# Mixture of 16,384 single-neuron experts: dense products with the whole tables, replaced by gathered rows per block of 128 tokens

## The chip, the cores and the metric

The kernel runs on one core of a Trainium2 chip. Its engines are TensorE (PE; products and transposes, results to PSUM), VectorE (DVE), ScalarE (ACT), GpSimd (POOL) and SyncE (SP, which here only issues DMAs); 16 DMA engines move data between HBM and SBUF. The metric is the device time of one execution in microseconds; the median of three runs before the change is 5664.9 us (5652.19 to 5668.03).

## The reference, cut to what matters

One layer of a backbone with 128 context tokens and 512 latent tokens, each of 2048 channels in float32. A token mixer (input projection, state-space scan, two convolutions, merge, output projection) is followed by PEER, a mixture of 16,384 experts of one neuron each. The change is in PEER:

```python
q = (xt @ p["peer_w_q"]).reshape(tok, PEER_HEADS, 2, PEER_QDIM // 2)   # 8 heads, two halves of 128
s1 = einsum("thd,nd->thn", q[:, :, 0], peer_k1)     # 128 first keys
s2 = einsum("thd,nd->thn", q[:, :, 1], peer_k2)     # 128 second keys
v1, i1 = top_k(s1, 16);  v2, i2 = top_k(s2, 16)
cand = v1[..., :, None] + v2[..., None, :]          # 256 sums a head
cidx = i1[..., :, None] * 128 + i2[..., None, :]    # expert = 128 * first key + second key
top, sel = top_k(cand.reshape(tok, 8, 256), 16)
idx = take_along_axis(cidx, sel);  g = softmax(top)
# per token: 8 heads x 16 = 128 experts
act = einsum("cd,ckd->ck", xc, u_tab[idx])          # u_tab, v_tab: [16384, 2048]
out = einsum("ck,ckd->cd", g * gelu(act), v_tab[idx])
```

The result is gated, added to the residual and normalised.

## The kernel before, in words

The token mixer comes first (`start`, `project`, `merge`); the change leaves it alone. `peer` (L1294) then works through blocks of 128 tokens: block 0 is the context, blocks 1 to 4 are the latents. Blocks 2, 3, 4 go as one group and 1, 0 as another through the output projection (`wo`, L933), the residual and LayerNorms (`norms`, which transposes the experts' input at L290) and the queries (`queries`, L610 and the scores at L973). Float32 products are made of three: an operand is split into a rounded part (h, ScalarE) and the rest (l, VectorE or GpSimd), and h·h, h·l and l·h are summed. `piece` (L165 to L175) loads 4 KB a partition of a weight and splits it (L173, L174).

`choose` (L1009) takes, for a block, the top 16 keys of each half (L1003 to L1007), the top 16 of their sums and the softmax (to L1048). For latents it then spreads the weights over all experts by products of one-hot rows: 64 steps of two tokens each (L1075 to L1095), into G in DRAM, [32, 16, 128, 128], in four writes of 2 MB a block (L1082).

For the latents, the experts are dense: for each first key e, `up` multiplies all 512 latents with the 128 rows of U of that key (48 products of 512 columns, L610) and takes the gelu; `weigh` multiplies by G; `down` (L1198) adds W^T V for four first keys at a time (L1210), 16 accumulations in PSUM that VectorE adds to `acc` (L1216). Fifty of the 128 `up` steps run ahead, beside the choosing (AHEAD). For the context, `gathers` (L1112) fetches one expert row a token and step by an indirect DMA that GpSimd issues (L1108), 128 rows of U and then of V, and VectorE does the arithmetic (L1124, L1131). `finish_context` and `finish_latents` end it.

The order on each engine comes from a scheduler that goes by the order of the program and its own estimates of time; it may put an instruction that is ready ahead of an earlier one that is not. Waits stand in each engine's instruction stream, in order.

Of the kernel before, what the change touches and what calls it, by code (L numbers as in the profile page):

```python
# [6 lines left out]
F32 = mybir.dt.float32  # L7
# [9 lines left out]
D = 2048  # L17
KT = 16
# [7 lines left out]
# columns of the constants  # L26
C_ID, C_IOTA, C_LOW, C_UP, C_ONES = 0, 128, 256, 384, 512
C_N = 640

# [39 lines left out]
def layout(i):  # L69
    """The device arrays: slices, transposes and copies of the inputs, and constants."""  # L70
# [3 lines left out]
    o["cst"] = consts()  # L74
    o["pos"] = grid_pos()
# [36 lines left out]
    o["put"] = A(n["peer_u"][0].reshape(128, 128, 2, 8, 128).transpose(0, 2, 4, 3, 1))  # L112
# [3 lines left out]
# steps of the gathered experts after each key of a group  # L116
UPS = (2, 2, 1, 0)
# after which pieces of the first adaLN weights the steps of the input come: a block's LN0 (b) and its turning (t),
# the parameters of S5 (p), a quarter of the projection's input and the first products with it (q)
# [4 lines left out]
class Quarters(list):  # L124
    """A tensor [128, 16, NT] in four tiles."""
# [6 lines left out]
class Kern:  # L132
# [8 lines left out]
    # ---- pools  # L141
# [22 lines left out]
    # ---- weights: raw piece of 4 KB a partition, its rounded part and the exact rest  # L164
# [16 lines left out]
    # ---- adaLN vectors; seq 0 is the context, seq 1 the latents  # L181
# [16 lines left out]
    def mod_chunk(self, n, ps, rp=None, tag="m", tb=4):  # L198
        """512 columns of the adaLN vectors; yields between its parts."""
# [37 lines left out]
    def late_mod(self, ps):  # L237
        """The vectors that the input projection does not need, in parts between its products."""
# [3 lines left out]
    # ---- 1/sqrt(var + eps) on DVE and ACT with one Newton step  # L242
# [15 lines left out]
    def ln_stats(self, pool, x):  # L258
        """The mean and 1 / deviation of the rows x [128, 2048]."""
# [8 lines left out]
    def ln_rows(self, pool, x, out):  # L268
        """out = LN0(x) for rows x [128, 2048]."""
# [3 lines left out]
    def x_rows(self, pool, b, x):  # L273
        """Block b of the layer's input into x: context, or latents with their grid positions."""
# [8 lines left out]
    def modulate_T(self, pool, ps, xn, seq, v, h, l, t0, tag, tb):  # L283
        """h, l [128, 16, t] at t0: the split of (xn * (1 + sc) + sh)^T; v is the index of sh."""
# [17 lines left out]
    def start(self):  # L302
# [5 lines left out]
        # LN0 of the input, transposed, by quarters of the channels; its modulated form, split, takes the rest of  # L308
        # the room and then that of the quarters that are done
# [59 lines left out]
        # shift and scale of a quarter of the channels, then that quarter of the projection's input  # L369
        # and of its first products; a chunk is finished under the next one's products  # L370
# [53 lines left out]
    def cmul(self, P, out, a, b, shape, tag, eng=None):  # L424
        """out = a * b for [128, 2, ...] complex tiles (given as (re, im) pairs)."""
# [12 lines left out]
    def s5_params(self, P):  # L438
# [18 lines left out]
        # sin and cos with the angle brought into [-pi, pi]  # L457
# [17 lines left out]
        # PW[e + 4] = a^e for e = -4 .. 11  # L475
# [16 lines left out]
        # z = (a - 1) / lambda  # L492
# [20 lines left out]
        # a^8 twice, the starting slots of the latents and a^3  # L513
# [8 lines left out]
        # powers by position in the chunk: for B, for C inside the chunk, for C on the state  # L522
# [6 lines left out]
        # scratch in DRAM, by blocks of 4 groups  # L529
# [64 lines left out]
    # ---- input projection: 128 columns of it, transposed, into two PSUM tiles of 320 tokens  # L594
# [6 lines left out]
    def mm_T(self, acc, hl, xh, xl, cols, kpp, fill=None):  # L601
        """acc[n] (128 columns, tokens) = sum over the pieces of w^T x, three products a term."""
# [15 lines left out]
    # the two sequences side by side with zeros around them, for depthwise convolutions  # L618
# [6 lines left out]
    def conv(self, P, t, pad, taps, w, bias, name, eng):  # L625
        """Depthwise convolution over the padded tokens; the gap between the sequences holds rubbish."""
# [7 lines left out]
    def times(self, out, acc, g):  # L634
        """out (the two padded sequences) = acc * g."""
# [5 lines left out]
    def conv_branches(self, P, ps):  # L641
        """The Conformer branch and the short one, a quarter of the channels at a time."""
# [8 lines left out]
        for j in range(4):  # L651
# [16 lines left out]
            # the long convolution has time; the products' operands go first  # L668
# [4 lines left out]
        # LayerNorm over the 512 channels, which lie on partitions  # L673
# [23 lines left out]
    # ---- S5 over chunks of 8 tokens; 16 + 64 chunks  # L697
    def s5_in(self, P, ps, j):
        """Groups 8j .. 8j+7: chunk inputs U, spilled, and what each chunk adds to the state."""
# [19 lines left out]
        for h in range(2):  # L719
# [3 lines left out]
            for r in range(2):  # L723
# [3 lines left out]
                # forward rows one slot up, backward rows one slot down  # L727
# [216 lines left out]
    def norms(self, blocks, X, T, ps):  # L944
        """x1, spilled, and the modulated input of the experts, transposed and split."""
        nc = self.nc
        for b in blocks:
# [5 lines left out]
            if b:  # L953
                continue
# [449 lines left out]
```

## Time and profile before

| | us or share |
|---|---|
| median of three executions | 5664.9 us |
| the profiled execution: span (its own time is not shown beside it) | 5655.2 us |
| TensorE busy | 5329.3 us, 94% |
| VectorE busy | 3745.6 us, 66% |
| ScalarE busy | 1618.9 us, 29% |
| GpSimd busy | 1198.4 us, 21% |
| moved by DMA | 1047.07 MB, 185 GB/s on average |

The span goes from the first instruction of the profiled execution to its last. Busy shares are means over stages that have different limits: the token mixer to about 2160 us, the choosing from about 2230 to 3250 us, the dense products to the end. A busy TensorE is an engine with a product in flight; how fast products follow each other is read from the start times in the timeline.

### The profile page before, as it was taken

How to read it: one execution, taken by the hardware profiler on the slowest of the kernel's cores; microseconds unless marked ns; L12 is line 12 of the kernel's file. 1: busy time of each engine (PE TensorE's matmuls, PEld its weight loads, DVE VectorE, ACT ScalarE, POOL GpSimd, SP SyncE). 2: the span in 40 equal slices, each digit the busy share in tenths (PEclk: the TensorE clock that was granted, in tenths of full speed). 3: DMA queues.
4: the chain of work that ended last, by engine and by line, in shares of the span. 5: the costliest groups of instructions: out<-in, count | busy, mean ns of one | idle time of the engine just before them, and what ended most of it. 6: DMA issues, size and time to landing. Idle time of an engine off the chain costs nothing.

```text
span 5655.2 us, 69883 instructions
## 1 busy us (share of the span) xinstructions
PE 5329.3 (94%) x27340; PEld 4518.4 (80%) x27340; DVE 3745.6 (66%) x5624; ACT 1618.9 (29%) x2214; POOL 1198.4 (21%) x914
## 2 busy tenths in 40 slices
PE   8999899999999989878888899999999999999998
PEld 3799789999999868866666687777777777777776
DVE  6782772666345475588888836666666666667667
ACT  3324334332232233332222232222222222222222
POOL 2000780000000145543323301111111111111113
PEclk9999999999999999999999999999999999999999
DMA  6544346554254654343443456667666677677663
GB/s 242 191 164 140 127 155 220 177 172 134 83 169 145 220 160 155 117 131 114 131 123 118 138 188 233 236 235 246 233 233 231 235 246 241 237 243 241 243 232 129
DMA packets 382763, 1047.07 MB, mean 185 GB/s; under 512 B 38464, under 2 KB 116672, under 8 KB 346464
## 3 DMA queue, kind: packets, MB, share of 16 engines
q1 hardware_dynamic: 253680, 669.41, 37.3%
q0 software_dynamic: 37840, 274.55, 13.2%
q10 hardware_dynamic: 90912, 98.64, 5.2%
q8 instruction: 215, 3.52, 0.3%
q14 instruction: 116, 0.95, 0.1%
HBM read 939.59 MB, written 102.89 MB: 184 GB/s over the span
## 4 chain that ended last, share of the span: by engine, by line
issue 24%; PE 19%; DVE 11%; DMA 6%; POOL 3%; ACT 1%; POOLq 0%; ACTq 0%; DVEq 0%
PE u L610 9%; PE v L1210 5%; DMA gr<-in_pv,idx 3%; POOL gr L1108 3%; PE a L610 2%; DVE dd L1095 2%; DVE oh L1090 2%; DMA G_d<-Gs 2%; PE g L1075 1%; DVE gy L1131 1%; PE a L933 1%; DVE Gs L1080 1%; DVE wl L174 0%; DVE x L999 0%; DVE bst L263 0%
## 5 line engine op out<-in xcount | busy, mean ns | idle before, releaser
L173 ACT CAST wh<-wr 128x1024 fp32r<-128x1024 f32 x793 | 833.1, 1051 | 2586.3 <-PE v L1210 862.1
L174 DVE TENSOR_TENSOR wl<-wr,wh 128x1024 fp32r<-128x1024 f32 x685 | 841.1, 1228 | 964.0 <-ACT wh L173 961.4
L610 PE MATMUL u<-hl,wh 128*128 128x512 f32 x2048 | 818.2, 400 | 0.0
L610 PE MATMUL u<-hh,wh 128*128 128x512 f32 x2048 | 817.0, 399 | 0.0
L610 PE MATMUL u<-hh,wl 128*128 128x512 f32 x2048 | 815.2, 398 | 0.0
L610 PE MATMUL a<-h,wl 128*128 128x320 f32 x2368 | 548.5, 311 | 18.6 <-DVE wl L174 18.6
L1210 PE MATMUL v<-wl,hh 128*128 128x512 f32 x1344 | 539.2, 401 | 27.0 <-DVE wl L174 27.0
L610 PE MATMUL a<-h,wh 128*128 128x320 f32 x2368 | 546.8, 312 | 0.0
L610 PE MATMUL a<-l,wh 128*128 128x320 f32 x2368 | 543.8, 310 | 0.0
L1210 PE MATMUL v<-wh,hh 128*128 128x512 f32 x1344 | 536.0, 399 | 1.8 <-ACT hh L1174 1.8
L1210 PE MATMUL v<-wh,hl 128*128 128x512 f32 x1344 | 536.7, 400 | 0.0
L610 PEld LDWEIGHTS u<-hh,wh 128*128 128x128 f32 x2048 | 389.8, 190 | 89.7
L610 PEld LDWEIGHTS u<-hh,wl 128*128 128x128 f32 x2048 | 389.2, 190 | 88.7
L610 PEld LDWEIGHTS u<-hl,wh 128*128 128x128 f32 x2048 | 389.1, 190 | 87.1
L610 PEld LDWEIGHTS a<-h,wl 128*128 128x128 f32 x2368 | 399.0, 189 | 20.8 <-DVE wl L174 20.1
L610 PEld LDWEIGHTS a<-h,wh 128*128 128x128 f32 x2368 | 403.2, 189 | 12.1
L1216 DVE TENSOR_TENSOR acc<-acc,v 128x512 f32<-128x512 f32 x496 | 332.9, 682 | 109.5 <-PE v L1210 105.3
L610 PEld LDWEIGHTS a<-l,wh 128*128 128x128 f32 x2368 | 398.3, 189 | 0.8
L174 POOL TENSOR_TENSOR wl<-wr,wh 128x1024 fp32r<-128x1024 f32 x108 | 279.0, 2583 | 500.3 <-ACT wh L173 486.7
L1108 POOL DMA_INDIRECT gr<-in_pu,idx x128 | 171.3, 1338 | 964.9 <-DVE gr L1124 939.0
L1108 POOL DMA_INDIRECT gr<-in_pv,idx x128 | 162.4, 1269 | 883.6 <-DVE gy L1131 852.5
L1210 PEld LDWEIGHTS v<-wl,hh 128*128 128x128 f32 x1344 | 255.9, 190 | 96.7 <-DVE wl L174 35.2
(396 smaller groups left out, 9397.4 us busy)
## 6 DMA issues: line engine op xcount, KB each, us to landing
wr<-in_pv SPq DMA_DIRECT2D x248, 512.0 KB
wr<-in_put SPq DMA_DIRECT2D x206, 512.0 KB
wr<-in_wmod SPq DMA_DIRECT2D x152, 512.0 KB
wr<-in_win SPq DMA_DIRECT2D x83, 512.0 KB
wrx<-in_win SPq DMA_DIRECT2D x69, 512.0 KB
G_d<-Gs ACTq DMA_DIRECT2D x16, 2048.0 KB
wrx<-in_put SPq DMA_DIRECT2D x50, 512.0 KB
wrx<-in_wmod SPq DMA_DIRECT2D x40, 512.0 KB
```

Of the source, the lines that this page charges most:

```text
L173: nc.scalar.copy(h, raw)
L174: (eng or nc.vector).tensor_sub(l, raw, h.bitcast(F32))
L610: nc.tensor.matmul(a, w, x[:, kt, c0:c0 + n], start=kt == 0 and i == 0, stop=kt == nk - 1 and i == 2)
L933: nc.tensor.matmul(acc[n, b], m[:, 2 * kp + k, b * 128:b * 128 + 128], w[:, k, :], start=kp + k + q == 0, stop=kp == 7 and k == 1 and q == 2)
L1075: i = nc.tensor.matmul(p[:, j], oh[:, 1, j], dd[:, j], start=True, stop=True)
L1080: v.tensor_add(s, s, p[:, :, 1].rearrange("j t i -> j i t"))
L1090: i = v.tensor_tensor(oh, self.iota[:, None, None, :].to_broadcast(sh), it[:, 0:2, t][:, :, :, None].to_broadcast(sh), op=ALU.is_equal)
L1095: v.tensor_mul(dd, oh[:, 0].bitcast(F32)[:, :, None, :].to_broadcast(sh), gr[:, t][:, :, :, None].to_broadcast(sh))
L1108: self.nc.gpsimd.indirect_dma_start(out=r, out_offset=None, in_=self.I[table], in_offset=bass.IndirectOffsetOnAxis(ap=self.idx[:, s:s + 1] ...
L1131: i = nc.vector.scalar_tensor_tensor(y, r, ga[:, q:q + 1], y, op0=ALU.mult, op1=ALU.add)
L1210: nc.tensor.matmul(a, w, x, start=m == 0, stop=m == 11)
L1216: i = nc.vector.tensor_add(y, y, a)
```

## The change

Every block, the context too, now has a list of its own. `choose` spreads the weights of a block over all experts into G_d[b] (one row of 128 tokens for each of 16,384 experts, and a row of zeros), counts for each expert whether any weight is above zero, and makes a list of the chosen experts: on each partition 16 rounds of the eight largest numbers give that partition's experts in order, L_d[b] holds them, and products with triangular matrices give the places of the entries, so that `entries` can fetch them 128 at a time with an indirect DMA. The list ends in experts whose weight row is the row of zeros. `choose` is a generator: block i+1 is chosen between the steps of block i's chunks.

`chunk` works on 256 listed experts of a block: the rows of U (4 indirect DMAs for U and V, 1 MB each) are transposed on TensorE in 8 steps, split, and multiplied with the block's 128 tokens, which are the stationary operand (48 products of 256 columns); the gelu is transposed, multiplied by the gathered rows of G and split; V's rows are split, and 24 products of 512 columns add to one accumulator in PSUM for the whole block. The second half of a chunk is done between the steps of the next. The first K0 = 24 chunks of a block run always; the other 40 stand in branches, each inside the one before, on the number of chosen experts. `finish` does the residual and LayerNorm of a block under the next block's first chunk. Dropped are the dense products, the run ahead, the context's own path and the row form of its input; the modulated input of all blocks is written to memory (h2_d) and read back by block, and the scores of all blocks but the first also. Docstrings and comments go too. Cut to its core:

```diff
-    XB = 5
+    XB = 4
@@ norms
-            self.modulate_T(T, ps, x, min(b, 1), 3, self.hh, self.hl, b * 128, "m", 2)
+            self.modulate_T(T, ps, x, min(b, 1), 3, self.hh, self.hl, b * 128, "a", 7)
+            for j, m in enumerate((self.hh, self.hl)):
+                nc.sync.dma_start(self.h2_d[b, j], m[:, :, t].bitcast(F32))
@@ choose, after the softmax
-        for n in range(64):            # two tokens a step: oh, dd [128, 2, 2, 128], two products
+        for n in range(32):
+            if n % 8 == 0:
+                st = T.tile([128, 128, 32], F32, name="Gs", tag="Gs", bufs=1)
+            oh = T.tile([128, 4, 128], F32, name="oh", tag="oa", bufs=2)
+            dd = T.tile([128, 4, 128], F32, name="dd", tag="od", bufs=2)
+            p = ps.tile([128, 4, 128], F32, name="g", tag="m", bufs=1)
+            for j in range(4):
+                k1, k2, w = (it[:, i, n * 4 + j:n * 4 + j + 1] for i in range(3))
+                v.tensor_scalar(oh[:, j], self.iota, k2, None, op0=ALU.is_equal)
+                v.tensor_scalar(dd[:, j], self.iota, k1, w, op0=ALU.is_equal, op1=ALU.mult)
+                nc.tensor.matmul(p[:, j], oh[:, j], dd[:, j], start=True, stop=True)
+            nc.scalar.copy(st[:, :, n % 8 * 4:n % 8 * 4 + 4], p.rearrange("j t i -> j i t"))
+            yield
+            if n % 8 == 7:
+                nc.scalar.dma_start(self.G_d[b][:NE].rearrange("(i j) t -> j i t", j=128)
+                                    [:, :, n // 8 * 32:n // 8 * 32 + 32], st)
+                v.tensor_reduce(cnt[:, n // 8], st, axis=AX.X, op=ALU.add)
+                yield
+        v.tensor_reduce(f, cnt.rearrange("p q i -> p i q"), axis=AX.X, op=ALU.add)
+        v.tensor_scalar(f, f, 0.0, None, op0=ALU.is_gt)
...
+        for r in range(16):
+            v.max(L[:, s], f)
+            if r < 15:
+                v.match_replace(f, L[:, s], f, 0.0)
+            if r % 4 == 3:
+                yield
@@ chunk
+        if c + 2 < NCH: self.entries(b, c + 2)
+        if c + 1 < NCH: self.gather_u(b, c + 1)
+        for g in range(8):
+            p = self.bank().rearrange("p (k e) -> p k e", k=2)
+            for k in range(2):
+                for j in range(2):
+                    nc.tensor.transpose(p[:, k, j * 128:j * 128 + 128],
+                                        self.ur[(2 * c + j) % 4][:, kt * 128:kt * 128 + 128], self.ident)
+            self.nc.scalar.copy(self.uh[g % 3], p)
+            nc.vector.tensor_sub(self.ul[g % 3], p, self.uh[g % 3].bitcast(F32))
+            if pending is not None:
+                if g == 0:
+                    self.weigh()
+                    self.gather_g(b, c)
+                for k in self.SPLITS.get(g, ()):       # {0: (0,), 1: (1,), 3: (2,), 5: (3,)}
+                    self.split_v(k)                    # k == 3: the subtraction on GpSimd
+                    if k % 2:
+                        self.gather_v(b, c, k // 2)
+            if g:
+                up(g - 1)
+            if pending is not None:
+                for u in self.DOWNS.get(g, ()):        # 8 parts of 3 products in steps 2 to 7
+                    self.down(u, pending)
+            yield
+        up(7)
+        nc.scalar.activation(self.t, self.a, AF.Gelu_apprx_tanh)
@@ experts
+        for i, b in enumerate(self.order):             # [2, 3, 4, 1, 0]
+            more = self.choose(self.order[i + 1]) if i < 4 else iter(())
+            self.gather_u(b, 0)
+            for c in range(K0):
+                for g, _ in enumerate(self.chunk(i, c, pending)):
+                    if g % 2:
+                        next(more, None)
+                if c == 0:
+                    if i: self.finish(i - 1)
+                    if i < 4: self.load_x(i + 1)
+                pending = c == 0
+            n = nc.values_load(self.lists[b]["count"][0:1, 2:3].bitcast(I32), min_val=0, max_val=NE, ...)
+            with contextlib.ExitStack() as st:
+                for c in range(K0, NCH):
+                    st.enter_context(tc.If(n > c * CH, name="more%d_%d" % (i, c)))
+                    for _ in self.chunk(i, c, False):
+                        pass
+            pending = False
+        self.last_chunk(pending)
+        self.finish(4)
```

## Rows read from the trace of the kernel before

**Rows 1.** The page: span, and each engine's busy time.

```profile
span 5655.2 us, 69883 instructions
PE 5329.3 (94%) x27340; PEld 4518.4 (80%) x27340; DVE 3745.6 (66%) x5624; ACT 1618.9 (29%) x2214; POOL 1198.4 (21%) x914
```

**Rows 2.** Stretches: length, busy PE PEld DVE ACT POOL, clock, DMA share, GB/s.

```profile
3500.00:4000.00 500.00, 491.25 (x2079) 393.38 (x2078) 332.15 (x366) 117.23 (x132) 78.86 (x59) 0.99 0.68 231
2600.00:2700.00 100.00, 83.19 (x368) 64.70 (x367) 93.35 (x231) 29.21 (x54) 30.79 (x12) 0.97 0.40 121
```

**Rows 3.** Chain of waits: shares by line; one piece (start, length).

```profile
by line: issue 23.6%; PE u L610 8.7%; PE v L1210 5.2%; DMA gr<-in_pv,idx 3.3%; POOL gr L1108 3.1%; PE a L610 2.4%; DVE dd L1095 2.2%; DVE oh L1090 2.0%; DMA G_d<-Gs 2.0%; PE g L1075 1.2%; DVE gy L1131 0.8%; PE a L933 0.7%; DVE Gs L1080 0.6%
...
2418.18 12.11 DMA G_d<-Gs
```

**Rows 4.** Timeline of PE, dense products: start, length, operation, idle before.

```profile
3711.82 0.40 PE L1210 MATMUL v<-wl,hh 128*128 128x512 f32 x1
3712.05 0.40 PE L1210 MATMUL v<-wh,hl 128*128 128x512 f32 x1
...
3716.03 0.79 PE L1210 MATMUL v<-wl,Wh 128*128 128x512 f32 x1 [3.35 <-DVE wl L174]
...
3717.05 0.63 PE L1210 MATMUL v<-wh,Wh 128*128 128x512 f32 x1
3717.47 0.63 PE L1210 MATMUL v<-wl,Wh 128*128 128x512 f32 x1
```

**Rows 5.** Timeline of PE: four transposes and what follows; 256-column products.

```profile
2196.04 0.60 PE L290 MATMUL tp<-cst,x 128*128 128x128 f32 x4
2196.39 0.42 PE L610 MATMUL a<-hh,wh 128*128 128x384 f32 x1
...
2427.67 0.28 PE L610 MATMUL a<-hh,wh 128*128 128x256 f32 x1
2427.79 0.28 PE L610 MATMUL a<-hl,wh 128*128 128x256 f32 x1
```

**Rows 6.** Groups on DVE: count, busy us, mean ns, idle before.

```profile
L174 DVE TENSOR_TENSOR wl<-wr,wh 128x1024 fp32r<-128x1024 f32 x685 | 841.1, 1228 | 964.0 <-ACT wh L173 961.4
L1216 DVE TENSOR_TENSOR acc<-acc,v 128x512 f32<-128x512 f32 x496 | 332.9, 682 | 109.5 <-PE v L1210 105.3
L1080 DVE TENSOR_TENSOR Gs<-Gs,g 128x256 f32<-128x256 f32 x256 | 104.4, 420 | 32.6 <-ACT Gs L1079 30.8
L1040 DVE TENSOR_REDUCE I<-oh 128x128 f32<-128x2048 f32 x10 | 22.8, 2278 | 0.0
```

**Rows 7.** Timeline of DVE: the first latent block's choosing.

```profile
2331.15 0.29 DVE L1003 MAX8 V<-S 128x8 f32<-128x128 f32 x1 [7.33 <-ACT S L976]
...
2353.66 0.22 DVE L1032 TENSOR_SCALAR au<-SE 128x128 uint32<-128x128 uint32 x1
2353.80 0.22 DVE L1033 TENSOR_SCALAR au<-SE 128x128 uint32<-128x128 uint32 x1
...
2373.20 0.68 DVE L1090 TENSOR_TENSOR oh<-cst,itT 128x512 fp32r<-128x512 f32 x1
...
2374.61 3.45 DVE L1095 TENSOR_TENSOR dd<-oh,gr 128x512 fp32r<-128x512 f32 x2
...
2389.78 1.28 DVE L1095 TENSOR_TENSOR dd<-oh,gr 128x512 fp32r<-128x512 f32 x2
```

**Rows 8.** Timeline of POOL at the same place.

```profile
2374.32 2.60 POOL L174 TENSOR_TENSOR wl<-wrx,wh 128x1024 fp32r<-128x1024 f32 x1 [1.14 <-ACT wh L173]
```

**Rows 9.** DMA: queue's packets, MB, share; issues, median us to landing.

```profile
q0 software_dynamic: 37840, 274.55, 13.2%
...
gr<-in_pu,idx POOLq DMA_INDIRECT x128, 7.5
```

**Rows 10.** Groups on POOL.

```profile
L1108 POOL DMA_INDIRECT gr<-in_pu,idx x128 | 171.3, 1338 | 964.9 <-DVE gr L1124 939.0 <-DVE wl L174 20.7 <-issue 4.6
```

**Rows 11.** DMA queues from 2418 to 2430 us, around one write of G.

```profile
q10 hardware_dynamic: 4112, 2.10, 64.6%
```

More of the change, by code (lines that the diff above doesn't have):

```diff
@@ L1 @@
+import contextlib
 import math
@@ L28 @@
 C_N = 640
+C_LS, C_LI, C_IDP, C_ONE = 0, 128, 256, 384
+CH = 256
+K0 = 24
+NCH = 64
+NE = 16384
 VERBOSE = False
@@ L921, in wo @@
         for n2 in range(2):
-            acc = {(n, b): ps.tile([128, 512], F32, name="a", tag="a", bufs=6) for n in range(2) for b in blocks}
+            acc = {(n, b): ps.tile([128, 512], F32, name="a", tag="a", bufs=7) for n in range(2) for b in blocks}
             for kp in range(8):
@@ L989, in queries @@
         scores(*last)
+        for b in blocks:
+            if b != self.order[0]:
+                nc.scalar.dma_start(self.S_d[b], S[b])
         return S
@@ new lines, in choose @@
+        nc.scalar.copy(oh[:, 3], p)
+        p = ps.tile([128, 128], F32, name="g", tag="m", bufs=1)
+        nc.tensor.matmul(p, self.cst(C_LI), oh[:, 2], start=True, stop=False)
+        nc.tensor.matmul(p, oh[:, 3], self.cst(C_LS), start=False, stop=True)
+        v.scalar_tensor_tensor(f, p, -1.0, self.cst(C_IDP), op0=ALU.add, op1=ALU.add)
+        si = T.tile([128, 128], I32, name="si", tag="si", bufs=2)
+        v.tensor_scalar(si, f, float(NE), None, op0=ALU.min)
+        self.lists[b] = dict(place=si, count=eu, rows=T.tile([128, 128], I32, name="ix", tag="ix", bufs=2),
+                             tab=T.tile([128, 128], I32, name="iu", tag="iu", bufs=2))
@@ new lines, in choose, with cst, indirect, entries @@
+        for c in range(2):
+            self.entries(b, c)
+        yield
+    def cst(self, c):
+        return self.cl[:, c:c + 128]
+    def indirect(self, out, table, idx):
+        self.nc.gpsimd.indirect_dma_start(out=out, out_offset=None, in_=table,
+                                          in_offset=bass.IndirectOffsetOnAxis(ap=idx, axis=0))
+    def entries(self, b, c):
+        l = self.lists[b]
+        for n in (2 * c, 2 * c + 1):
+            self.indirect(l["rows"][:, n:n + 1], self.L_d[b], l["place"][:, n:n + 1])
+        s = slice(2 * c, 2 * c + 2)
+        self.nc.vector.tensor_scalar(l["tab"][:, s], l["rows"][:, s], NE - 1, None, op0=ALU.min)
@@ new lines, in gather_u, with gather_v, gather_g, load_x @@
+    def gather_u(self, b, c):
+        for j in range(2):
+            self.indirect(self.ur[(2 * c + j) % 4], self.I["pu"], self.lists[b]["tab"][:, 2 * c + j:2 * c + j + 1])
+    def gather_v(self, b, c, j):
+        self.indirect(self.vr[j], self.I["pv"], self.lists[b]["tab"][:, 2 * c + j:2 * c + j + 1])
+    def gather_g(self, b, c):
+        for j in range(2):
+            self.indirect(self.gr[:, j], self.G_d[b], self.lists[b]["rows"][:, 2 * c + j:2 * c + j + 1])
+    def load_x(self, i):
+        for j in range(2):
+            self.nc.sync.dma_start(self.xs[i % 2][j].bitcast(F32), self.h2_d[self.order[i], j])
@@ new lines, in down, with bank @@
+    def down(self, u, first):
+        i, d = divmod(u, 2)
+        j, d = i // 2, i % 2 * 2 + d
+        s = slice(u % 2 * 512, u % 2 * 512 + 512)
+        h, l = self.vh[i % 3][:, s], self.vl[i % 3][:, s]
+        for n, (w, x) in enumerate(((self.Wh, h), (self.Wh, l), (self.Wl, h))):
+            self.nc.tensor.matmul(self.acc[:, d], w[:, j], x, start=first and j == 0 and n == 0, stop=j == 1 and n == 2,
+                                  skip_group_check=True)
+    def bank(self):
+        self.nbank += 1
+        return self.tb[self.nbank % 2]
@@ L1267, in finish_context, with last_chunk, finish @@
+    def last_chunk(self, pending):
+        self.nbank = 1
+        self.weigh()
+        for k in range(4):
+            self.split_v(k)
+            for u in (2 * k, 2 * k + 1):
+                self.down(u, pending)
+    def finish(self, i):
+        nc, b, F = self.nc, self.order[i], self.E
+        x = F.tile([128, D], F32, name="fx", tag="fx", bufs=1)
+        nc.sync.dma_start(x, self.x1_d[b])
         for n in range(4):
             s = slice(n * 512, n * 512 + 512)
-            nc.gpsimd.tensor_mul(y[:, s], y[:, s], self.rows(F, self.modr[0, 5:6, s], "r1"))
```

396 lines of the change are left out of this document (148 added, 248 removed).

## The prediction, made before the changed kernel ran

> **What bounds the kernel now.** I read four views, in this order. The page: TensorE is busy 94% of a span of 5655.2 us [rows 1]. The table by stretches: from 3500 to 4000 us, inside the experts' products, TensorE is busy 491 of 500 us at a granted clock of 0.99, VectorE 332; from 2600 to 2700 us, while experts are chosen, VectorE is busy 93 of 100 us and TensorE only 83 [rows 2]. The chain of waits: its largest named parts are the two product lines, L610 and L1210, and "issue" (time in which TensorE waits for nothing that is shown) [rows 3]. So the experts are bound by TensorE's own instructions, and the choosing by VectorE. Last the timeline, for the pace: from start to start a 128x512 product takes 0.234 us at full clock and 0.427 at the lower level, which follows a gap of 3.35 us [rows 4]. 12,288 dense products (128 first keys, 48 up and 48 down each) make 2875 us at that pace.
>
> **The change, part by part.** All times are in the profiled execution's frame. Its span is 5655.2 us; the three timed executions have a median of 5664.9, so I add 10 us for what lies around the span.
>
> How many chunks run: the choices are in the reference's inputs, so I counted the distinct experts with the reference's own routing: 6674, 6550, 6501 and 6608 for latent blocks 2, 3, 4, 1 and 7349 for the context. In chunks of 256 that is 27, 26, 26, 26 and 29, together 134; 24 of each block are unconditional, so 9 conditional chunks run in the first four blocks and 5 in the last.
>
> TensorE, one chunk: 24 down products of 512 columns at 0.234 us are 5.6; 48 up products of 256 columns at 0.12 (from start to start) are 5.8; 32 transposes of rows and 2 of weights at 0.09 (four begin within 0.35 us) are 3.1 [rows 4, 5]. Sum 14.4 us; 134 chunks are 1930 us against 2875. The weight load is hidden under each product in these rows.
>
> VectorE, one chunk: 8 subtractions of 512 columns at 0.68, 3 of 1024 at 1.23, one multiply of 256 at 0.42, two small ones 0.5: 10 us [rows 6]. Back to back each starts about 0.08 us before the other's end, which leaves 9.0. The fourth subtraction stands on GpSimd, and there the trace shows a price: two VectorE products that take 1.28 us together took 3.45 when a GpSimd subtraction of 2.60 us ran beside them [rows 7, 8]. I add 2.2: 11.2 us; bounds 9.0 and 11.2.
>
> Choosing, on VectorE, for one block: the part up to the softmax is in the trace whole, 2331.15 to 2373.20, 42 us, with all but the last key lists done before; those are 16 us more (16 lists at about 1.2, less three). Spreading the weights is now 256 operations of 128 columns; the nearest row starts 0.14 us apart and lasts 0.22 [rows 7]; I take 0.18, 46 us (36 to 56). Four counting reductions of 4096 elements, twice the 2.28 us of the row of 2048 [rows 6], are 18; 16 rounds of the list about 10; small ones 3. Sum 135 us. It is cut into 65 pieces, one after every second of a chunk's 8 steps, so it lasts 16.25 chunks at 8.3 us each: VectorE has 19.5 us in those, more than TensorE's 14.4. VectorE gets 93% busy in such a stretch [rows 2], so a chunk takes 21.0.
>
> A chunk with no choosing beside it: 14.4 plus a stall at its head. There VectorE has 4.6 us to do in the first two steps (two subtractions of 0.68, two of 1.23, the weights' 0.8), TensorE 1.6; I take 2.3 us of the 3.0 between them, as the schedule can move some: 16.7.
>
> Transfers: a chunk gathers 4.3 MB; the software queue moves 274.55 MB in 13.2% of 16 engines' span, 368 GB/s at best: 11.7 us, hidden [rows 9]. GpSimd issues 8 gathers at 1.34 [rows 10] and subtracts once: 13.3 us, hidden as well, but close. A V gather that is issued 8 to 9 us into a chunk lands 7.5 us later [rows 9], about when the next chunk wants it; if GpSimd is 2 us late, the chunk is.
>
> The weights' way through memory: the 2 MB writes of G now have runs of 128 bytes, 16,384 where there were 4096 of 512. In 12 us, 4112 packets took 64.6% of 16 engines: 30 ns each [rows 11]. By packets the new write takes 31 us, by bytes 8, by four times the old write's 12.11 [rows 3] 48. I take 31. Its tile has one buffer, so the next eight steps' copies on ScalarE wait for it. ScalarE runs in order: behind that wait are the copies that TensorE needs. In 12 places (three a block, four blocks) I take 8 us each, 96 in all, as most of a write can lie under steps in between; bounds 0 and 40.
>
> Until the first chunk: scores of the first blocks are ready at 2331. Choosing 42 us, then four quarters of 16 us (eight steps of 2 us: products, then the copy out of one PSUM buffer) with three writes between them, 30 each, then the list, its round trip and the first two gathers, 35: 2373 + 154 + 35 is about 2560 (2500 with writes of 8 us, 2611 with 48). The other blocks' queries run beside it, as they do now. The modulated input of all blocks goes to memory on SP's queue (10 MB, 27 us at 368 GB/s) with the weights of L933 and the queries behind it; TensorE there waits little, 0 to 15 us, taken as nothing.
>
> Conditional chunks: the trace has no branch. Bounds: nothing, and a full emptying (rows land 7.5 us after issue, first copy, subtraction and product 2, the last products 6: about 16). I take 4 a chunk that runs and 6 a branch that is skipped, nearer to nothing since each branch holds the next and rows are fetched a chunk ahead. End: last weights, splits, down products and one LayerNorm, 45 us.
>
> Sum: 2560 + 4 x (16.25 x 21.0 + 7.75 x 16.7) = 1880, + 30 for four blocks' LayerNorms (17 us of VectorE each, half hidden), + 96, + 24 x 16.7 = 401 for the last block, + 14 x 20.7 = 290, + 5 x 6 = 30, + 45: 5332; with the 10 us, 5340 us.
>
> **Rivals.**
> A, all that is shared hides. GpSimd doesn't hold VectorE up, writes take 8 us, branches 1: 2500 + 4 x (16.25 x 17.3 + 7.75 x 14.4) + 30 + 24 x 14.4 + 14 x 15 + 5 + 45, and 10: 4720 us. For it: TensorE is 98% busy with VectorE at 66% [rows 2]. Against it: the 3.45 us row, and VectorE's load in 65 of 134 chunks.
>
> B, slower: ScalarE stands at the G writes. If a write takes 48 us, and about 40 of it isn't covered because gathers share the engines, 12 waits cost 480 instead of 96, and the start moves by 51: 5780 us. It decides once a wait costs over 35 us (323 us of gain over 12, and the 8). For it: one buffer, an in-order engine, and the old write, four times fewer runs, already stands on the chain of waits [rows 3]. Against it: eight chunks of slack a block, so that the copies may be put late enough. The Trainium skill, "DMA: Bandwidth & Descriptors", Specifications, says that descriptors below 512 bytes make the engine read, modify and write; by it a write would be nearer 62 us than 31, and the sum near this rival's. No row here has such runs.
>
> C, slower: TensorE's stalls bring its clock down. The lower level came after a gap of 3.35 us [rows 4]. A chunk wholly at it is 14.4 x 0.427/0.234 = 26.3 us; half of the work there makes 20.3, with the head's 2.3 22.6: 134 of these, 2560 and the other terms make 5850 us. It decides from about 0.4 of the work. For it: chunks have stalls and many short instructions. Against it: with TensorE 83% busy the clock still was 0.97 [rows 2]. The Trainium skill, "TensorE: Matmul & The Clock Gate", Part 4, speaks against the change here: a transpose takes about 275 ns in a kernel and doesn't bring the full clock. By it 34 would be 9.4 us instead of 3.1, 20.7 a chunk, near this rival's sum. The row shows 88 ns [rows 5]; I go by the row.
>
> D, the branches don't do what they say cheaply: each of 14 conditional chunks runs with nothing beside it (16 us more) and each skip costs 20: 5332 + 14 x 12 + 5 x 14 + 10, 5580, and if what follows a skip also starts cold, as much again at most, 5820.
>
> **How the numbers follow.** Forecast 0.58 (its own range 5080 to 5630), A 0.12, B 0.15, C 0.08, D 0.07. Faster by over 0.3% (about what can be told from no change): 0.56 of the forecast, A, half of D and a little of B: 0.72. Within 0.3%: 0.04. Slower: most of B, C and a part of D: 0.24. The range leaves out the far half of A, C and the upper part of B: 4860 to 5780.
>
> **What would show it.** 134 gelu operations of 256 columns; first gather of U near 2550; chunks near 21 us while choosing runs and near 17 after, with VectorE over 90% busy in the first and about 65% in the second; down products 0.234 us apart and transposes 0.09; G writes near 31 us, ScalarE's idle before its copies into Gs near 100 us in all; no gap over 10 us at a branch. A wrong chunk period is what the sum is most exposed to: 1 us is 134 us. 2.4 us more and nothing is left of the gain.

## The result, and the profile after

The changed kernel takes 5933.7 us (median of 4 runs, 5930.9 to 5937.9) against 5658.6 before: a ratio of 1.049 with a 95% interval of 1.047 to 1.050. It is slower; 5340 was forecast, and the range ended at 5780.

The page after, with the lines that answer to [rows 1], the queues that answer to [rows 9, 11], and the clock by slices of 148 us:

```profile
span 5934.5 us, 78074 instructions
PE 4928.9 (83%) x30087; PEld 4380.6 (74%) x30087; DVE 3391.0 (57%) x6809; ACT 2165.5 (36%) x3212; POOL 2018.3 (34%) x1752
...
PEclk9999999999999889879889888888888888888888
...
q0 software_dynamic: 97392, 596.40, 28.4%
...
q10 hardware_dynamic: 347648, 101.59, 8.4%
```

TensorE has 400 us less to do and the kernel is 279 us longer: the gain in work is there, and more than that is lost in idle time, which grew from 326 us to 1006. Four stretches of it: two with choosing, one of the last block, where nothing is chosen, and one of that block's last chunks, which stand in branches (columns as in [rows 2]).

```profile
2700.00:2760.00 60.00, 45.81 (x259) 39.88 (x258) 33.08 (x58) 21.41 (x33) 25.95 (x22) 0.86 0.71 185
2880.00:2940.00 60.00, 37.74 (x240) 33.65 (x241) 34.62 (x80) 19.73 (x32) 15.42 (x13) 0.80 0.66 166
5300.00:5780.00 480.00, 394.14 (x2311) 337.94 (x2312) 217.51 (x302) 205.41 (x306) 186.71 (x152) 0.89 0.58 203
5806.00:5870.00 64.00, 61.06 (x385) 50.68 (x384) 36.80 (x54) 34.29 (x53) 44.79 (x32) 0.97 0.70 248
```

The reader is to see that in the third line no engine is near full, with no choosing there, and that in the fourth, the same work behind branches, TensorE is busy 61 of 64 us. From one gelu to the next (each chunk has one, 134 in all) it is about 21.8 us in the third and 17.1 in the fourth.

What ends the idle time, for ScalarE from 2500 us on (us in total, times, longest):

```profile
ACT uh L1251 <- PE tb L1249: 797.0, 539, 28.5
ACT wh L1204 <- DMA vr<-in_pv,iu: 425.6, 142, 7.1
ACT Gs L1095 <- DMA G_d<-Gs: 170.5, 10, 21.1
```

The first line is ScalarE waiting for TensorE, which costs nothing by itself. The second is 142 waits for gathered rows of V, the third the waits for writes of G. The chain of waits from 5400 to 5480 goes round through the second (start, length, what):

```profile
5421.23 1.06 ACT wh L1204
5422.36 2.41 POOL wl L1205
5425.03 5.20 DMA vr<-in_pv,iu
5430.27 1.05 ACT wh L1204
5431.35 1.23 DVE wl L1205
5433.23 1.29 PE a L1243 x5
5441.67 1.06 ACT wh L1204
5442.80 2.41 POOL wl L1205
5445.47 5.45 DMA vr<-in_pv,iu
```

A part of V is split, GpSimd makes its rest, only then can the next gather fill that buffer, and ScalarE stands until it lands. One turn is 20.4 us here. The timelines of ScalarE and then of GpSimd show where the planner put the splits (wh) in such a chunk:

```profile
5500.50 0.39 ACT L1268 ACTIVATE t<-a 128x256 f32<-128x256 f32 x1 [1.95 <-PE a L1243]
...
5508.60 1.05 ACT L1204 CAST wh<-vr 128x1024 fp32r<-128x1024 f32 x1 [0.35 <-PE acc L1214]
5509.78 0.59 ACT L1251 CAST uh<-tb 128x512 fp32r<-128x512 f32 x1
5511.13 1.05 ACT L1204 CAST wh<-vr 128x1024 fp32r<-128x1024 f32 x1 [0.77 <-PE acc L1214]
...
5514.12 0.59 ACT L1251 CAST uh<-tb 128x512 fp32r<-128x512 f32 x1 [1.45 <-PE tb L1249]
5518.79 1.04 ACT L1204 CAST wh<-vr 128x1024 fp32r<-128x1024 f32 x1 [4.08 <-DMA vr<-in_pv,iu]
5519.74 0.58 ACT L1251 CAST uh<-tb 128x512 fp32r<-128x512 f32 x1
5520.22 1.05 ACT L1204 CAST wh<-vr 128x1024 fp32r<-128x1024 f32 x1
5522.90 0.39 ACT L1268 ACTIVATE t<-a 128x256 f32<-128x256 f32 x1 [1.63 <-PE a L1243]
```

```profile
5509.72 2.40 POOL L1205 TENSOR_TENSOR wl<-vr,wh 128x1024 fp32r<-128x1024 f32 x1 [3.76 <-ACT wh L1204]
5512.39 1.90 POOL L1162 DMA_INDIRECT vr<-in_pv,iu  x1 [0.27 <-POOL wl L1205]
```

The split that GpSimd goes on with stands 8 us after the gelu (5508.60), so the gather behind it goes out at 5512.39. The split that needs those rows stands in the same chunk, ahead of its last U copy (5519.74): that copy, without which TensorE can't end the chunk, waits 4 us for a gather.

### The profile page after: what moved, and what is told of

The parts are those of the page before. It is cut to its first block, busy times and chain, and to the rows that moved or that the text cites. A ratio compares the mean times of both kernels' runs of the same rounds, so it can differ in the third digit from the quotient of the medians.

```text
span 5934.5 us, 78074 instructions
## 1 busy us (share of the span) xinstructions
PE 4928.9 (83%) x30087; PEld 4380.6 (74%) x30087; DVE 3391.0 (57%) x6809; ACT 2165.5 (36%) x3212; POOL 2018.3 (34%) x1752
## 5 line engine op out<-in xcount | busy, mean ns | idle before, releaser
L1252 DVE TENSOR_TENSOR ul<-tb,uh 128x512 fp32r<-128x512 f32 x1072 | 730.3, 687 | 597.3 <-ACT uh L1251 563.1
L1251 ACT CAST uh<-tb 128x512 fp32r<-128x512 f32 x1072 | 625.0, 586 | 884.4 <-PE tb L1249 797.0
L1243 PE MATMUL a<-uh,xh 128*128 128x256 f32 x2144 | 737.0, 344 | 230.7 <-ACT uh L1251 225.8
L1243 PE MATMUL a<-ul,xh 128*128 128x256 f32 x2144 | 691.4, 322 | 225.9 <-DVE ul L1252 212.9
L1249 PE MATMUL tb<-cst,ur 128*128 128x128 f32 x4288 | 746.6, 303 | 140.8 <-DVE ul L1252 93.7
L1204 ACT CAST wh<-vr 128x1024 fp32r<-128x1024 f32 x536 | 557.5, 1047 | 602.6 <-DMA vr<-in_pv,iu 425.6
L1249 PEld LDWEIGHTS tb<-cst,ur 128*128 128x128 f32 x4288 | 586.1, 156 | 232.3 <-DVE ul L1252 106.8
L1205 DVE TENSOR_TENSOR wl<-vr,wh 128x1024 fp32r<-128x1024 f32 x402 | 488.1, 1222 | 377.8 <-ACT wh L1204 370.1
L1243 PE MATMUL a<-uh,xl 128*128 128x256 f32 x2144 | 645.4, 301 | 0.0
L192 DVE TENSOR_TENSOR wl<-wr,wh 128x1024 fp32r<-128x1024 f32 x281 | 345.7, 1231 | 377.6 <-ACT wh L191 375.6
```

What stands on the lines that cost most here:

```text
L192: (eng or nc.vector).tensor_sub(l, raw, h.bitcast(F32))
L1204: nc.scalar.copy(h, src)
L1205: (nc.gpsimd if i == 3 else nc.vector).tensor_sub(l, src, h.bitcast(F32))
L1243: nc.tensor.matmul(self.a, x[:, kt], w[:, k], start=kt + n == 0, stop=kt == 15 and n == 2)
L1249: nc.tensor.transpose(p[:, k, j * 128:j * 128 + 128], self.ur[(2 * c + j) % 4][:, kt * 128:kt * 128 + 128], self.ident)
L1251: self.nc.scalar.copy(self.uh[g % 3], p)
```

## The experiments

Theory: the chunks' period is set by the order that the planner gave them, together with V's single buffers; the G writes and the end of a block add to it. Rivals: TensorE's clock, the load of choosing on VectorE, the DMA engines, the branches. The mean times between gelus, in us, from the timelines (with choosing: chunks 2 to 17 of the first four blocks; without: their chunks 18 to 23; start: a block's first two periods together; in the runs e9 and e10 the choosing goes on into chunks 18 to 23):

```
run                         time    with   without  conditional  last block  start
changed kernel            5933.7    25.9    22.4       18.8         21.8      77.4
e1_last_in_branches       5769.5    25.8    21.1       17.2         17.1      73.9
e2_long_runs              5729.8    23.6    22.6       18.5         21.8      69.0
e3_v_after_u              5591.2    21.5    19.7       22.7         17.1      89.1
e4_all_in_branches        5525.8    23.8    17.1       17.1         17.1      70.4
e5_two_g_tiles            5409.4    21.8    17.2       17.2         17.1      73.6
e6_norm_in_pieces         5487.0    24.1    17.1       17.3         17.1      63.3
e7_both                   5352.9    22.0    17.1       17.2         17.2      63.2
e8_both_long_runs         5302.7    21.6    17.2       17.2         17.2      63.6
e9_three_a_chunk          5400.0    21.6    20.7       17.1         17.2      61.3
e10_three_from_chunk_2    5384.0    20.7    22.3       18.4         17.3      58.0
e11_rounded_products      5339.4    21.9    17.2       17.2         17.1      63.7
e12_rounded_from_chunk_2  5340.6    21.9    17.7       17.3         17.2      59.0
```

**Order, one block.**

```diff
-            for c in range(K0):
+            k0 = K0 if i < 4 else 1
+            for c in range(k0):
...
-                for c in range(K0, NCH):
+                for c in range(k0, NCH):
...
-                    for _ in self.chunk(i, c, False):
+                    for _ in self.chunk(i, c, c == 1):
```

> Same work; the last block's chunks 1 to 23 now stand in branches of their own, as its chunks 24 to 28 did, so each engine meets them in the order of the program text. In the changed kernel these chunks are 22.5 us apart and the ones in branches 17.1. Theory (in the planned order ScalarE stands at the split of V's rows before the U copies that TensorE needs): 23 x (22.2 - 17.1) = about 115 us less, near 5815, with ScalarE's waits for the gathered V rows gone from that block. Rival (TensorE's clock, or the DMA engines, set 22 us): nothing changes, 5920 to 5945. Rival (a branch costs more when there are more of them): above 5945.

Measured 5769.5, 164 less. From the last gelu before it to its own last one, the last block went from 630.8 us to 514.7: 116 less, the theory's number (11 of them in its first two periods). (The other blocks, planned anew, lost 66 more, and the end grew by 22.) ScalarE in one of these chunks:

```profile
5606.60 0.38 ACT L1268 ACTIVATE t<-a 128x256 f32<-128x256 f32 x1 [1.68 <-PE a L1243]
5606.88 1.04 ACT L1204 CAST wh<-vr 128x1024 fp32r<-128x1024 f32 x1
5607.81 0.59 ACT L1251 CAST uh<-tb 128x512 fp32r<-128x512 f32 x1
5608.29 0.42 ACT L1196 CAST Wh<-w 128x256 fp32r<-128x256 f32 x1
5608.60 1.06 ACT L1204 CAST wh<-vr 128x1024 fp32r<-128x1024 f32 x1
5609.55 0.60 ACT L1251 CAST uh<-tb 128x512 fp32r<-128x512 f32 x1
5610.02 1.07 ACT L1204 CAST wh<-vr 128x1024 fp32r<-128x1024 f32 x1
5610.97 0.61 ACT L1251 CAST uh<-tb 128x512 fp32r<-128x512 f32 x1
5612.35 1.05 ACT L1204 CAST wh<-vr 128x1024 fp32r<-128x1024 f32 x1 [0.77 <-PE acc L1214]
```

Here the splits start 0.3 us after the gelu and are done 6.8 us after it; none waits for a gather, and the next has the rest of the chunk to land. From 5240 to 5700 us ScalarE waits for V's rows no more, and over the whole run 317.7 us and not 425.6. One thing in the expectation was wrong: this isn't the order of the text (which has the fourth split at step 5); the planner orders inside a branch too, but only one chunk at a time. The stretch of the block, 5240 to 5700 us:

```profile
5240.00:5700.00 460.00, 440.34 (x2850) 365.74 (x2849) 257.29 (x377) 241.25 (x377) 343.86 (x242) 1.00 0.71 254
```

TensorE is 96% busy at the full clock, and 28 nested branches cost nothing that shows. So the clock of 0.89 before was an effect of the stalls and not their cause.

**The same without branches.**

```diff
-        nc.scalar.copy(h, src)
-        (nc.gpsimd if i == 3 else nc.vector).tensor_sub(l, src, h.bitcast(F32))
+        a = nc.scalar.copy(h, src)
+        d = (nc.gpsimd if i == 3 else nc.vector).tensor_sub(l, src, h.bitcast(F32))
+        if self.after:                      # the step's own uh copy and ul subtraction
+            self.pause(a, self.after[0])
+            if i != 3:
+                self.pause(d, self.after[1])
...
-            self.nc.scalar.copy(self.uh[g % 3], p)
-            nc.vector.tensor_sub(self.ul[g % 3], p, self.uh[g % 3].bitcast(F32))
+            self.after = (self.nc.scalar.copy(self.uh[g % 3], p),
+                          nc.vector.tensor_sub(self.ul[g % 3], p, self.uh[g % 3].bitcast(F32)))
```

`pause` puts an instruction behind another of its engine, for the order alone.

> No branches more than before; the split of V's rows is held, on ScalarE and VectorE, behind the U copies of the step that it is written in. Theory (the place of the V split in the planned order costs about 5 us in each of the chunks without a branch): last block 22.5 to about 17.5 us a chunk, the others 25 to about 20, 24 x 5 + 96 x 5 = 600 us less, near 5340. Rival (V's gather is late whatever the order, because its tile has one buffer): last block stays at 21 to 22, total within 60 us of 5934. Rival (the choosing on VectorE sets the choosing blocks): only the last block gains, near 5815.

Measured 5591.2, 343 less, where 600 was expected. The last block's planned chunks fell from 21.8 to 17.1 with V's single buffers kept, and of ScalarE's 425.6 us of waits for V's rows none is left, so the rival of the one buffer falls: the order alone does it. Chunks with choosing fell by 4.4; in the second block seven of them with one piece of choosing each (its chunks 3 to 5 and 7 to 10) take 17.2 to 17.3 us. Against that, conditional chunks rose by 4 us: GpSimd waits about 5 us in each for the pinned split, with the next chunk's gathers behind it. The block starts grew by 12, which stays open.

**Everything in branches.** All chunks but each block's first; the choosing's tiles are taken once and used in turn.

```diff
-            for c in range(K0):
+            for c in range(1):
...
-                for c in range(K0, NCH):
+                for c in range(1, NCH):
                     st.enter_context(tc.If(n > c * CH, name="more%d_%d" % (i, c)))
-                    for _ in self.chunk(i, c, False):
-                        pass
+                    steps(c, c == 1)        # the chunk, and a piece of choosing after every second step
```

> All chunks but each block's first stand in branches, so the choosing too goes in the order of the text, a piece after every second step; its tiles are fixed ones in turn. Theory (order): the last block gains 115; chunks with choosing fall from 25 to about 21, those of the block after it to 17.1: 115 + 4 x (16 x 4 + 7 x 6) = about 540 less, near 5400, the waits at the G writes still there. Rival (VectorE's choosing and the G writes set the choosing blocks, not the order): 115 to 250 less, 5680 to 5820. Rival (in the order of the text the choosing's own waits now stand ahead of the U splits): slower than the run with only the last block in branches.

Measured 5525.8, 408 less and 0.977 (0.976 to 0.979) of the kernel before. All chunks with no choosing are now at 17.1, and ScalarE's waits for V's rows are gone; chunks with choosing are at 23.8, where 21 was expected and the pinned order had 21.5. No run puts the mends that follow on the pinned order.

**G's runs.**

```diff
-                nc.scalar.dma_start(self.G_d[b][:NE].rearrange("(i j) t -> j i t", j=128)
-                                    [:, :, n // 8 * 32:n // 8 * 32 + 32], st)
+                nc.scalar.dma_start(self.G_d[b][n // 8 * 4096:n // 8 * 4096 + 4096].rearrange("(j r) t -> j (r t)", j=128),
+                                    st.rearrange("j i t -> j (i t)"))
```

> The weights G are written in runs of 16 KB and so land in other rows than the gather takes them from: the weights are the wrong ones, the work otherwise the same. Theory (the 128-byte runs hold ScalarE at the next weights' tile, 177 us of waits in all, and make the four or five chunks of 33 to 44 us in each choosing block): these chunks fall to about 25, 180 us less, near 5750. Rival (those waits lie beside other waits): under 50 us less, 5880 to 5930. Rival (the DMA engines are the bound of the whole choosing part): 300 us less or more.

Measured 5729.8, 204 less: the theory's size. Of it 37 us lie before the first chunk. ScalarE's waits for G fell from 170.5 us to 84.0. In the changed kernel one write, issue to the copy that stood behind it:

```profile
2889.62 0.37 ACTq L1098 DMA_DIRECT2D G_d<-Gs  x1
2911.62 0.59 ACT L1095 COPY Gs<-g 128x512 f32<-128x512 f32 x1 [20.73 <-DMA G_d<-Gs]
```

**A second tile for G** (16 KB beside the first; LayerNorm's input lies in it between times), on top of the run with everything in branches:

```diff
                 st = T.tile([128, 128, 32], F32, name="Gs", tag="Gs", bufs=1)
+                if b != self.order[0] and n // 8 % 2:
+                    st = self.big.rearrange("p (i t) -> p i t", t=32)
```

> As the run with all chunks in branches (5525.8), with a second tile of 16 KB for the weights, which LayerNorm's input shares when the weights don't need it. Theory (the 128-byte runs cost because ScalarE stands, 154.5 us in 12 waits there, until the tile has been written): the three chunks of 36 us in each choosing block fall to about 24, 12 x 12 = 140 less, near 5385. Rival (they cost because 65536 small packets a block fill the DMA engines and make the gathered rows late): under 40 us less, 5485 to 5525.

Measured 5409.4, 116 less; of the waits for G (154.5 us before) 5.7 are left, and the chunks of 36 us are at 22 (one in a block stays at 30). The rival falls for the most part.

**LayerNorm in pieces**, on top of the run with everything in branches. There VectorE stood at the end of the old block as follows:

```profile
4955.36 0.69 DVE L1305 TENSOR_TENSOR gy<-acc,r 128x512 f32<-128x512 f32 x1 [0.50 <-DMA r<-modr]
4959.74 0.69 DVE L1305 TENSOR_TENSOR gy<-acc,r 128x512 f32<-128x512 f32 x1 [3.69 <-DMA r<-modr]
4969.49 1.29 DVE L1306 SCALAR_TENSOR_TENSOR fx<-fx,gy 128x512 f32<-128x512 f32 x2 [9.06 <-DMA fx<-x_d]
```

```diff
+            fin = self.finish(i - 1) if i else iter(())
+            next(fin, None)                 # asks for x and four rows of the gate
...
                     if g % 2:
                         next(more, None)
+                    elif c:
+                        next(fin, None)     # statistics, then a quarter of the LayerNorm each
```

> As the run with all chunks in branches (5525.8); the end of a block (gate, residual, LayerNorm) asks for its input and four rows of 512 before the next block's first chunk and goes in pieces between the steps of chunks 1 and 2. Theory (VectorE stands for these loads ahead of the weights and U's rests; the first two periods of a block are 62 to 78 us there, against 34): about 25 us less at each of four boundaries, near 5425. Rival (the new block's U rows come late because their gather is issued only behind the last branch): 5500 or more.

Measured 5487.0, 39 less, where 100 was expected. The block starts gained 7 us each, not 25, and the end of the kernel 29; the chunks with choosing lost 0.3 each. So the waits for loads were only a part of what a block start costs; the time lies nearer to the rival's 5500.

**Both.** Here, and in the two runs with one of them, a branch of the first 24 chunks asks `n > 0`, which always holds, so that nothing rests on how many experts a block chose.

> The second weights tile and the LayerNorm in pieces together. If both theories hold and they lie in different chunks: 5525 - 140 - 100 = about 5285. If one falls, the sum of the other and 5525: 5385 or 5425.

Measured 5352.9 (5347.1 to 5359.7): 0.946 (0.945 to 0.948) of the kernel before, 581 less than the changed one, 173 less than with branches alone, where the two by themselves gave 116 and 39 (the tile alone had made the block starts longer, 73.6 against 70.4).

A part of what a block's start still costs lies behind the branches (L1366). The fourth block's last gelu starts at 4783.19; then, on TensorE and GpSimd:

```profile
4786.55 0.66 PE L1215 MATMUL tb<-cst,t 128*128 128x128 f32 x2 [3.40 <-ACTq L1366]
4787.01 0.94 POOL L1183 DMA_INDIRECT ur<-in_pu,iu  x1 [9.40 <-PEq L1366]
4790.33 0.80 PE L1235 MATMUL acc<-wh,Wh 128*128 128x512 f32 x1 [3.13 <-ACT Wh L1217]
4794.35 0.63 PE L1270 MATMUL tb<-cst,ur 128*128 128x128 f32 x2
```

The new block's rows of U are asked for only behind the branches, so TensorE stands 6.5 us and begins the old chunk's second half with nothing beside it. This start, with no choosing, takes 59.2 us; the three others, with choosing, take 61.9 to 66.1.

**Both, and long runs.**

> As the run before it, the weights written in runs of 16 KB and so into other rows than the gather reads: the weights are the wrong ones. If what the short runs cost is only that ScalarE stood for the tile, nothing is left to gain: within 20 us of the run before. If their packets also hold up the gathered rows: 60 to 150 us less, since in the scheduled chunks long runs gave 204.

Measured 5302.7, 50 less: between the two. 26 of it lie before the first chunk, where the first block's choosing has one tile still; beside the chunks short runs cost little once nobody stands for their tile.

**The choosing, thinner or later**, on top of the run with both.

```diff
-                    if g % 2:
+                    if g % 3 == 1:          # the second run: c > 1 and g % 3 == 1
```

> As the run with both (5352.9), the choosing a piece after every third step, three a chunk and not four, so it lies beside some 22 chunks and not 16. If a chunk's 17.1 us have room on VectorE (about 6 us beside its own 11) and only what goes over it counts: 16 x 4.7 = 75 us a block of choosing seen now become 22 x 1.5 = 33, 120 to 170 less, near 5200. If each piece costs the chunk the same wherever it lies (ScalarE and TensorE stand behind it in the order): within 20 us of 5353.

> As the run before it, the choosing held back until chunk 2, so that LayerNorm has the chunks 0 and 1 alone. Where VectorE was busy 72.7 of 75 us at a block's start, the first two periods (31 + 31) fall to about 25 + 22: 4 x 12 = 50 us less than the run before. If the new block's U rows set them (their gather is issued only behind the last branch): within 15 us of it.

Measured 5400.0 and 5384.0: 47 and 31 more than with four pieces. The theory of free room fell. Where the weights are spread, four pieces make a chunk 21.8 us and three 20.9, that is 4.7 and 3.8 over 17.1: about 1.2 us a piece in either. The products of a piece hold TensorE as long (4.96 us for four, below). Holding the choosing back until chunk 2 gave 16 us, a third of what was expected and about what the rival had.

**The choosing's products.** In the run with both, these were 19.1 of 100 us of TensorE.

```diff
-            oh = T.tile([128, 4, 128], F32, name="oh", tag="oa", bufs=2)
-            dd = T.tile([128, 4, 128], F32, name="dd", tag="od", bufs=2)
+            oh = T.tile([128, 4, 128], F32R, name="oh", tag="oa", bufs=2)
+            dd = T.tile([128, 4, 128], F32R, name="dd", tag="od", bufs=2)
```

> As the run with both (5352.9), but the products that spread the weights take their one-hot rows and weights in TensorE's rounded float32 (each weight is rounded once, its rest left out). In that run they held TensorE 19.1 of 100 us, 4.2 in each chunk of 21.8, beside 17.1 for the chunk itself. Theory (TensorE bounds these chunks too, and the choosing's products are what they add): 16 products of 128 columns at the transposes' 0.09 are 1.4 instead of 4.2, so the eight chunks fall to about 19, 4 x 8 x 2.8 = 90 less, near 5265. Rival (VectorE, busy 80 of 100 us there, with the waits of its order): they stay at 21 to 22 and the time within 15 us of 5353.

> As the run before it, the choosing held back until chunk 2 so that LayerNorm has chunks 0 and 1 alone. With three pieces a chunk this gave 16 us. If VectorE's load at a block's start is what is left there: 15 to 30 less than the run before. If the late U rows are: within 10 us.

Measured 5339.4 and 5340.6: 13 and 12 less than with both, where 90 was expected. The kernel before took 5659.0 us beside the run with both and 5645.1 beside these two, so the ratios to it (0.9464, and 0.9450 and 0.9455, each give or take 0.0016) don't tell the three apart. The second run's block starts are 4.6 us shorter, and later chunks lost that again. One chunk with four pieces, with both (first fence) and with rounded products (second), each with all engines and then the choosing's products and copies alone:

```profile
3935.57:3957.33 21.76, 20.55 (x140) 17.64 (x139) 16.85 (x40) 11.01 (x18) 10.07 (x9) 1.00 0.57 199
...
3935.57:3957.33 21.76, 4.96 (x32) 4.33 (x32) 0.00 (x0) 2.35 (x4) 1.00 0.57 199
```

```profile
3933.15:3954.00 20.85, 18.90 (x124) 15.75 (x123) 17.34 (x42) 11.04 (x18) 10.11 (x9) 1.00 0.59 211
...
3933.15:3954.00 20.85, 2.96 (x16) 2.47 (x16) 0.00 (x0) 2.36 (x4) 1.00 0.59 211
```

At the same granted clock the products gave 2.0 us back, where 2.8 was expected, and the chunk 0.9. With both, TensorE is busy 94% of such a chunk (96% of a plain one), and the chunk is 4.7 us over a plain one for 5.0 of products; with rounded products it is 3.7 over for 3.0. So TensorE set these chunks for a part, and with cheaper products something else does. Chunks with three pieces and a G write gained nothing (29.8 and 30.1), and over chunks 2 to 17 the mean went from 22.0 to 21.9. That the rest is the loop from transpose to copy to rest, with a piece's eight VectorE operations in it, is argued, not shown.

## Why the prediction was wrong

**What held.** 134 chunks. The work: TensorE's chunk was forecast at 16.7 us with the stall at its head, and is 17.1 wherever the order lets it. The pace of products, in a branch after (start, length):

```profile
5829.68 0.39 PE L1214 MATMUL acc<-wh,Wh 128*128 128x512 f32 x1
5829.91 0.40 PE L1214 MATMUL acc<-wl,Wh 128*128 128x512 f32 x1
...
5831.08 0.60 PE L1249 MATMUL tb<-cst,ur 128*128 128x128 f32 x4
5831.44 0.36 PE L1243 MATMUL a<-uh,xh 128*128 128x256 f32 x1
```

0.23 us apart as in [rows 4], four transposes in 0.36 as in [rows 5]. The Trainium skill, "TensorE: Matmul & The Clock Gate", Part 4, has a transpose at about 275 ns and short of the full clock. The first is near what one lasts here, 303 ns in the mean of the changed kernel's 4288, but the next starts after 90, so 34 cost 3.1 us and not 9.4. Against the second the granted clock was 1.00 over 460 us, with 34 of them among 72 products in every chunk; transposes alone are in no run.

**The step that failed** is "A chunk with no choosing beside it: 14.4 plus a stall at its head", 16.7. It took the engines' loads and let "the schedule" place the rest at no price. The planned chunks without choosing took 22.4 and 21.8. The working had named the place (a V gather "lands 7.5 us later [rows 9], about when the next chunk wants it; if GpSimd is 2 us late, the chunk is") and then gave it no term and no rival. It had the gather issued 8 to 9 us into a chunk; in the chunk above it went out at 11.9. The experiments show the price: about 5 us for each planned chunk, gone, with the 425.6 us of waits for V's rows, when the splits of V stand elsewhere on ScalarE.

Over the whole sum, by the times between gelus:

- Chunks with choosing: 25.9 against 21.0 and the G waits' 1.5: 64 x 3.4, +218. Of the 64, 16 take 29.6 to 44 us, the other 48 take 21.9 in the mean, so the surplus lies in the long ones. Long G runs took 150 us off the 64, the pinned order 283.
- Planned chunks without: 24 x 5.7 and 22 x 5.1: +249. With the first line this is where most of the error is: the price of the order, and the G writes' term, which was too small.
- Block starts: 77.4 against 55.5 (two of 21.0, 7.5 for LayerNorm, 6 for skipped branches): +88. VectorE's waits for LayerNorm's loads are a part (7 of the 36 us over two plain chunks that are left with branches), and the stand behind the branches is another (6.5 in the run with both); what the rest is stays open.
- The first gelu at 2624, not 2577 (2560 and a chunk): +47; long G runs take 37 of it away.
- Conditional chunks 18.8, not 20.7: -27. The end 41.8, not 51 (45, and 6 for the last block's skipped branch): -9.

That is +566 of the 602 by which the span missed the sum. Most of the rest, 34, is this list's own: it has 73 chunks at 21.0 where the sum has 65.

**VectorE's load in choosing chunks.** Forecast: 93% busy, so 21.0. In the changed kernel VectorE was busy 33 to 35 of 60 us there: it was waiting. With both mends a chunk is 22.0, so the term's size was right for a kernel that gets its order right, by a reason that the runs don't bear out: where the weights are spread VectorE is busy 16.9 of 21.8 us and TensorE 20.5 (the fence above). The sum gave the choosing's products no time on TensorE; they hold it 1.2 us a piece, and that is what a piece costs in the branches. In the pinned order a chunk with one piece cost 0.1 to 0.2 over a plain one, so this price too hangs on the order.

**G writes.** Forecast 31 us each, ScalarE idle 96 in all. Measured 22 and 170.5. The mechanism of rival B is there, at a third of B's price: a second tile gave 116 us back. The Trainium skill, "DMA: Bandwidth & Descriptors", Specifications, says that descriptors below 512 bytes are read, modified and written. By that I had 62 a write; 22 is below even the 31 by the packets of [rows 11], though nearly twice the 12.11 of four times fewer runs [rows 3]. From 2889 to 2912 us the write's queue took 75.6% of 16 engines for 16,400 packets: 17 ns each, where the working had 30 for a packet of any size.

**Rivals C and D.** The clock did fall, to 0.89 in the last block, and rose to 1.00 when the order changed with the same products: a follower. Entering a branch cost nothing that shows, and branches help where the plan had the splits late; leaving a block's branches cost the 6.5 us above, near the 6 of the sum.

With the order, the tile and LayerNorm mended the time is 5352.9, 0.2% from the forecast of 5340: it had priced the work and left out the order. That it comes so close is luck in part: 14 conditional chunks at 17.2 and not 20.7 (-49) pay for block starts of 63.2 and not 55.5 (+31) and a first gelu at 2595 and not 2577 (+18).

## What to carry to other kernels

When a planner orders the instructions, a sum of engine loads is a lower bound: take every single-buffered gather and ask which in-order engine will stand for its landing, what is queued behind, and give that a term with a rival. When no engine is near full and the same wait on a DMA comes back once a turn, change the order before anything else; cutting the plan into small pieces can be enough. Look at one chunk before you say what sets it: the run with both, from 3340 to 3440 us, has TensorE at 85% and a clock of 0.97, but the chunk with four pieces has 94% at 1.00; and taking 2.0 us from the fuller engine there gave 0.9.

## What the runs showed of the hardware that was not expected

- A 2 MB write in 16,384 runs of 128 bytes took 22 us beside gathers (2889.62 to 2911.62), less than twice the 12.11 of the write with 4096 runs: 17 ns a packet against 30.
- Up to 28 branches inside each other were entered in a block, and chunks stayed at 17.1 us: entering one cost no time that the gelus show. Leaving them at a block's end, TensorE stood 6.5 us.
- A granted clock of 1.00 over 460 us with TensorE 96% busy, and 0.89 with 82%, for the same instructions.
